# A hybrid encoder layer on one core: the feed-forward stage as a list of steps in a written order

## The chip, the cores and the metric

The kernel runs on one core of one Trainium2 chip. The metric is the device time of one execution in microseconds, as the median of several runs. The engines are named as the profile names them: PE (TensorE; its weight loads are a row of their own, PEld), DVE (VectorE), ACT (ScalarE), POOL (GpSimd) and SP (SyncE, which here only issues transfers). "PEclk" is the share of its full clock that TensorE was granted.

## The reference, cut to what matters

One layer works on a sequence of 256 tokens of width 2048, all in float32. First comes a mixer of two attention groups, whose output is added to x. Then the feed-forward part, which the change is about:

```python
def conv_ffn(h, w_up_l, conv_w_l, conv_b_l, w_down_l):
    u = h @ w_up_l                                   # 2048 -> 2 * 5632
    u = depthwise_causal_conv(u, conv_w_l) + conv_b_l  # width 3, one filter per column
    gate, val = jnp.split(u, 2, axis=-1)
    return (jax.nn.silu(gate) * val) @ w_down_l      # 5632 -> 2048

h = rms_norm(x, ffn_norm)
x = x + conv_ffn(h, w_up, conv_w, conv_b, w_down)
```

The convolution adds, for each column and token, that token's value and the two tokens' before it, each times a weight of the column: three taps and a bias.

## The kernel before, in words

**Two numbers for one.** TensorE multiplies a rounded form of float32 (`float32r`). To keep the precision, every operand is held as a high part (rounded) and a low part (the rest), and a product is made of three: high by high, high by low, low by high. So each weight tile of 1 MB (128 partitions by 2048 values) is loaded into a raw buffer (`load`, L198), cast to its high part on ScalarE (L208), and its low part is the difference of the two, on VectorE (L209). `split` (L204) does the last two. In the feed-forward stage there are four raw buffers and three each for the high and low parts.

**Up pieces and products.** In the up projection two 128-column tiles of `w_up` (a pair) are multiplied by all of h. A pair takes two up pieces, each with one weight tile: eight steps of k, in each two matmuls of 512 columns (L252, high weights by h's high and low part side by side) and two of 256 (L257, low weights by h's high part). The pair's accumulator `pu` comes from a pool of two. When it is complete, `summed` adds its two halves (copy on ScalarE at L268, addition on VectorE at L269), L603 scales the tokens into `up`, and the three taps follow: the last one with the bias on ScalarE (L607), the other two as fused multiply-and-add on VectorE (L612), for each 128-row half alone, so four per pair. When gate and value are both there, SiLU (L783), their product (L784), its high part g (L786) and low part (L787) follow.

**Parts.** The 44 tiles of gate (and of value) are cut into a first part of four tiles and five of eight (`FFN_PARTS`). A part of eight takes 16 up pieces. While one part goes through the up projection, the down projection of the part before runs between its up pieces. For the first part and the last it is done plainly (`down_plain`). For the four parts between, it is done by a scheme of seven products instead of eight (`down_in_seven`, L666): for each of two blocks of 1024 output columns, seven products of 12 matmuls each (L683), so 14 per part. It needs sums and differences of weight tiles (`w_sum`, L715, L722, L728, L739, on VectorE) and of blocks of gate times value (`combinations`, L644: four operations of 256 columns at L652 to L655 on tiles of tag t2, then a high part at L657 and a low part at L658). Each product's result is added to x at once (L692). These four parts' products run during the up projections of the parts after them, which are called loaded parts here. After the last part comes its own down projection, eight pieces of 24 matmuls (L760 to L762), with additions to x (L766) and the stores.

**What sets the order.** Only TensorE's instructions are in the order of the program (L772). On the other queues a scheduler chooses the order from its own cost model and from priorities: `weights` and the down products' loads and splits are moved ahead by 200 instructions (`AHEAD`), the readouts and the work on gate and value by 400. How many products stand between the up pieces is set by a pace, 14 of 16 in the loaded parts but 4 of 16 for the first plain part:

```python
        pace = 4 if n_part == 1 else 14
        for f in range(f_lo, f_hi, 2):
            gate = up_pair(f, "gate", 3, f == f_hi - 2)
            val = up_pair(NFT + f, "val", 1, f == f_hi - 2)
```

What is left of the products at a part's end is emitted before the next part begins.

**The start of the stage.** x is complete when the last output projection has been added (L564). Its last 512 columns are transposed and split into hT (L148, L153, L154, in `next_rows`) by a generator that `step()` advances after each up piece, and h's scale per token (`rstd2`) is applied only later, at L603.

**Projections.** Before the feed-forward stage, `token_major` (L222) makes the products of the attention projections and of the output projection, with three matmuls (L237, L238, L239) per k and token tile in the order high by high, high by low, low by high.

Of the kernel before, what the change touches and what calls it, by code (L numbers as in the profile page):

```python
# [14 lines left out]
P = 128  # L15
D = 2048
# [27 lines left out]
def hybrid_layer(  # L44
# [176 lines left out]

    def token_major(lhs, w, k0, nk, c0, cols, pieces=None, before=None):  # L222

        acc = psa.tile([P, NT, 512], F32, name="acc", tag="acc")
        k = 0
        for n in pieces or [4] * (nk // 4):
            if before:
                before(k, n)
            hi, lo = weights(rows_of(w, k0 + k, n, c0, cols), n, cols)
            for i in range(n):  # L230
                first, last = k + i == 0, k + i == nk - 1
                lh = lhs(k + i)
                for t in range(NT):
                    lhi = lh[:, 0, t * P : (t + 1) * P]
                    llo = lh[:, 1, t * P : (t + 1) * P]
                    o = acc[:, t, :cols]
                    nc.tensor.matmul(o, lhi, hi[:, i, :], start=first, stop=False)  # L237
                    nc.tensor.matmul(o, lhi, lo[:, i, :], start=False, stop=False)  # L238
                    nc.tensor.matmul(o, llo, hi[:, i, :], start=False, stop=last)  # L239
            k += n  # L240
            step()
        return acc
# [330 lines left out]
    R = None  # L573
# [15 lines left out]
    n_up = 0  # L589

    def convolution_parameters():
# [4 lines left out]

    def convolved(ps, f0, tag, bufs):

        nonlocal n_up
        u = up[n_up % 2]  # L600
        n_up += 1
        t2 = summed(ff, ps, "t2")
        dve.tensor_tensor(u[:, :, 2:], t2, R.unsqueeze(1).to_broadcast([P, 2, S]), op=ALU.mult)  # L603
        a = ff.tile([P, 2, S], F32, name=tag, tag=tag, bufs=bufs)
        for j in range(2):
# [5 lines left out]
            for w in range(2):  # L611
                dve.scalar_tensor_tensor(  # L612
                    a[:, j, :], u[:, j, w : w + S], ccol[:, w, f : f + 1], a[:, j, :],
                    op0=ALU.mult, op1=ALU.add,
                )
        return a


    behind = deque()
    n_behind, pace = 0, 0  # L620

    def step():
        nonlocal n_behind
        for g in list(waiting):
            if next(g, g) is g:
                waiting.remove(g)
        n_behind += pace
        while behind and n_behind >= 16:
            if next(behind[0], behind) is behind:
                behind.popleft()  # L630
            else:
                n_behind -= 16

    def up_pair(f0, tag, bufs, soon):

        nonlocal R
        acc = feature_major(wu, f0 * P, psa, "acc")
        if R is None:
            R = in_every_partition(dg2, 2, const)
            convolution_parameters()  # L640
        with tc.high_priority(offset=2 * AHEAD) if soon else nullcontext():
            return convolved(acc, f0, tag, bufs)

    def combinations(g1, g2):  # L644


        a11, a21 = g1[:, :, :P], g1[:, :, P:]
        a12, a22 = g2[:, :, :P], g2[:, :, P:]
        s = ff.tile([P, 2, 4, 2, P], F32R, name="s", tag="s")
        t = [ff.tile([P, 2, 2, P], F32, name="t2", tag="t2") for _ in range(2)]  # L650
        t5, s2, s4, t7 = t[0][:, 0], t[0][:, 1], t[1][:, 0], t[1][:, 1]
        dve.tensor_tensor(t5, a21, a22, op=ALU.subtract)  # L652
        dve.tensor_tensor(s2, t5, a11, op=ALU.subtract)
        dve.tensor_tensor(s4, a12, s2, op=ALU.add)
        dve.tensor_tensor(t7, a11, a21, op=ALU.subtract)  # L655
        for i in range(2):
            act.copy(s[:, 0, 2 * i : 2 * i + 2], t[i])  # L657
            dve.tensor_tensor(  # L658
                s[:, 1, 2 * i : 2 * i + 2], t[i], f32(s[:, 0, 2 * i : 2 * i + 2]), op=ALU.subtract
            )  # L660
        return s

    def store(t, c0):
        nc.sync.dma_start(of[t * P : (t + 1) * P, c0 : c0 + 512], xt[t][:, c0 : c0 + 512])

    def down_in_seven(f0, pairs, sums, c0):  # L666


        w11, w12 = (rows_of(wd, f0, 4, c0 + i * 512, 512) for i in range(2))
        w21, w22 = (rows_of(wd, f0 + 4, 4, c0 + i * 512, 512) for i in range(2))  # L670

        def of_pairs(h, t):
            return lambda a, part, j: pairs[2 * h + a][:, part, j, t * P : (t + 1) * P]

        def of_sums(q):
            return lambda a, part, j: sums[a][:, part, q, j, :]

        def product(bank, first, lhs, parts):
            hi, lo = parts
            for i in range(4):  # L680
                a, j = divmod(i, 2)
                for n, (l, r) in enumerate(((0, hi), (0, lo), (1, hi))):
                    nc.tensor.matmul(  # L683
# [4 lines left out]
        def add(t, half, bank, op=ALU.add):  # L688
            c = c0 + 512 * half
            to = xt[t][:, c : c + 512]  # L690
            with tc.high_priority(offset=2 * AHEAD):
                dve.tensor_tensor(to, to, bank, op=op)  # L692
# [168 lines left out]
```

## Time and profile before

| | us |
|---|---|
| median of 3 runs (1159.28 to 1160.48) | 1160.47 |
| the profiled execution | 1159.43 |
| its span, first to last instruction | 1157.7 |
| TensorE busy | 1123.5 |
| VectorE busy | 888.9 |
| ScalarE busy | 608.2 |
| moved by DMA | 219.77 MB, mean 190 GB/s |

A line of a group or of the timeline names the program's line, the engine, the operation, and out<-in by tile name. In the timeline the first number is the start and the second the length, with the engine's idle time before it in brackets and what ended that. In a table of stretches each row is a stretch of the span, its length, the busy time of PE, PEld, DVE, ACT and POOL with the number of instructions, the granted clock, the share of the DMA engines and their rate. A line of waits is: who <- for whom, total us, how often, the longest. A busy TensorE is not TensorE at its peak, since the end of a matmul is modelled; its rate is read from start to start.

### The profile page before, as it was taken

The numbers are of one execution on the slowest core, as the hardware profiler recorded it, in microseconds if no ns is written. First come the engines' busy times: TensorE is split into PE (matmuls) and PEld (weight loads), VectorE is DVE, ScalarE is ACT, GpSimd is POOL, SyncE is SP. The second block draws the span as 40 slices with busy tenths as digits, with TensorE's granted clock in tenths as the row PEclk, the third lists the DMA queues.
The fourth block names the chain that finished last, engine by engine and source line by source line (L and its number), as shares of the span: only waits on it lengthen the run. The fifth ranks groups of instructions, "written<-read, shape, count | busy, mean of one in ns | idle before, by whom it ended". The sixth has DMA issues, their size and how long they took to land.

```text
span 1157.7 us, 14490 instructions
## 1 busy us (share of the span) xinstructions
PE 1123.5 (97%) x5906; PEld 964.0 (83%) x5906; DVE 888.9 (77%) x972; ACT 608.2 (53%) x664; POOL 0.2 (0%) x4
## 2 busy tenths in 40 slices
PE   7999999999999989999999998999899998999988
PEld 6998888888888878888888887888788887888866
DVE  5646656555465676777899998999999999999983
ACT  5644445345564555554555555465655565565551
POOL 0000000000000000000000000000000000000000
PEclk9999999999999999999999998999999999999999
DMA  7666545555444395555557573665856565576641
GB/s 235 206 217 197 182 147 182 164 164 166 158 150 147 107 309 178 195 197 183 183 182 242 194 242 122 213 224 182 267 168 209 193 218 182 182 255 207 230 163 55
DMA packets 166763, 219.77 MB, mean 190 GB/s; under 512 B 3864, under 2 KB 117674, under 8 KB 166698
## 3 DMA queue, kind: packets, MB, share of 16 engines
q1 hardware_dynamic: 166698, 218.86, 58.1%
q8 instruction: 46, 0.75, 0.3%
q14 instruction: 19, 0.16, 0.0%
HBM read 216.75 MB, written 2.10 MB: 189 GB/s over the span
## 4 chain that ended last, share of the span: by engine, by line
PE 92%; DVE 3%; ACT 2%; DMA 1%; issue 1%; SPq 0%; DVEq 0%; ACTq 0%
PE pu L252 33%; PE pu L257 16%; PE acc L238 7%; PE acc L237 7%; PE acc L239 7%; PE bank_a L683 7%; PE bank_b L683 4%; PE bank_c L683 2%; ACT w_hi L208 2%; DVE w_lo L209 2%; PE acc L760 1%; PE acc L761 1%; PE acc L762 1%; PE bank_a L760 1%; PE bank_a L761 1%
## 5 line engine op out<-in xcount | busy, mean ns | idle before, releaser
L209 DVE TENSOR_TENSOR w_lo<-w_raw,w_hi 128x2048 fp32r<-128x2048 f32 (+2 forms) x204 | 449.6, 2207 | 193.4 <-ACT w_hi L208 192.6
L208 ACT CAST w_hi<-w_raw 128x2048 fp32r<-128x2048 f32 (+2 forms) x204 | 375.8, 1842 | 326.3 <-PE pu L252 103.4
L252 PE MATMUL pu<-hT,w_hi 128*128 128x512 f32 x1664 | 528.5, 399 | 14.4 <-DVE t L269 13.4
L257 PEld LDWEIGHTS pu<-hT,w_lo 128*128 128x128 f32 x1664 | 315.4, 190 | 76.3 <-DVE w_lo L209 2.0
L257 PE MATMUL pu<-hT,w_lo 128*128 128x256 f32 x1664 | 329.3, 279 | 1.5 <-DVE w_lo L209 1.5
L252 PEld LDWEIGHTS pu<-hT,w_hi 128*128 128x128 f32 x1664 | 260.3, 191 | 20.5 <-issue 14.6
L237 PE MATMUL acc<-w_hi,hT 128*128 128x512 f32 (+1 forms) x320 | 119.9, 375 | 0.0
L238 PE MATMUL acc<-w_lo,hT 128*128 128x512 f32 (+1 forms) x320 | 119.0, 372 | 0.8 <-DVE w_lo L209 0.8
L239 PE MATMUL acc<-w_hi,hT 128*128 128x512 f32 (+1 forms) x320 | 118.6, 371 | 0.0
L208 ACT CAST w_hi<-w_sum 128x2048 fp32r<-128x2048 f32 x24 | 45.9, 1914 | 79.9 <-DVE w_sum L715 43.4
L238 PEld LDWEIGHTS acc<-w_lo,hT 128*128 128x128 f32 x320 | 60.4, 189 | 9.9 <-DVE w_lo L209 1.7
L239 PEld LDWEIGHTS acc<-w_hi,hT 128*128 128x128 f32 x320 | 60.4, 189 | 8.7
L237 PEld LDWEIGHTS acc<-w_hi,hT 128*128 128x128 f32 x320 | 60.5, 189 | 8.2
L209 DVE TENSOR_TENSOR w_lo<-w_sum,w_hi 128x2048 fp32r<-128x2048 f32 x24 | 54.9, 2290 | 3.2 <-ACT w_hi L208 2.8
L683 PE MATMUL bank_a<-w_hi,g 128*128 128x512 f32 x128 | 42.1, 390 | 0.0
L683 PE MATMUL bank_b<-w_hi,s 128*128 128x512 f32 x128 | 42.1, 390 | 0.0
L683 PE MATMUL bank_a<-w_hi,s 128*128 128x512 f32 x128 | 42.1, 390 | 0.0
L612 DVE SCALAR_TENSOR_TENSOR val<-up,ccol,val 128x256 f32<-128x256 f32 x88 | 38.1, 480 | 0.2
L268 ACT COPY t<-pu 128x512 f32<-128x512 f32 x52 | 30.2, 580 | 15.1 <-PE pu L257 14.2
L612 DVE SCALAR_TENSOR_TENSOR gate<-up,ccol,gate 128x256 f32<-128x256 f32 x88 | 37.5, 479 | 0.7 <-ACT gate L607 0.7
L237 PE MATMUL acc<-w_hi,oT 128*128 128x512 f32 x96 | 38.0, 396 | 0.0
L239 PE MATMUL acc<-w_hi,oT 128*128 128x512 f32 x96 | 37.5, 390 | 0.0
(186 smaller groups left out, 1172.9 us busy)
## 6 DMA issues: line engine op xcount, KB each, us to landing
w_raw<-in_w_up_dram SPq DMA_DIRECT2D x88, 1024.0 KB, 5.5
w_raw<-in_w_down_dram SPq DMA_DIRECT2D x52, 1024.0 KB, 5.2
w_raw<-in_w_in_dram SPq DMA_DIRECT2D x36, 1024.0 KB, 5.3
w_raw<-in_w_out_dram SPq DMA_DIRECT2D x16, 1024.0 KB, 5.3
w_raw<-in_w_in_dram SPq DMA_DIRECT2D x12, 688.0 KB, 4.2
w_raw<-in_w_in_dram SPq DMA_DIRECT2D x8, 512.0 KB, 4.2
out_dram<-x SPq DMA_DIRECT2D x8, 256.0 KB, 2.4
x<-in_x_dram SPq DMA_DIRECT2D x3, 512.0 KB, 6.2
```

What stands on the lines that cost most here:

```text
L208: act.copy(hi[:, :n], raw[:, :n])
L209: dve.tensor_tensor(lo[:, :n], raw[:, :n], f32(hi[:, :n]), op=ALU.subtract)
L237: nc.tensor.matmul(o, lhi, hi[:, i, :], start=first, stop=False)
L238: nc.tensor.matmul(o, lhi, lo[:, i, :], start=False, stop=False)
L239: nc.tensor.matmul(o, llo, hi[:, i, :], start=False, stop=last)
L252: nc.tensor.matmul(acc[:, j, :], hi[:, i, j * P : (j + 1) * P], hT[:, k].rearrange("p a b -> p (a b)"), start=k == 0, stop=False,)
L257: nc.tensor.matmul(acc[:, j, S:], lo[:, i, j * P : (j + 1) * P], hT[:, k, 0, :], start=False, stop=k == KT - 1,)
L268: act.copy(t2, acc[:, :, S:])
L612: dve.scalar_tensor_tensor(a[:, j, :], u[:, j, w : w + S], ccol[:, w, f : f + 1], a[:, j, :], op0=ALU.mult, op1=ALU.add,)
L683: nc.tensor.matmul(bank, lhs(a, l, j), r[:, i, :], start=first and i + n == 0, stop=i == 3 and n == 2, skip_group_check=not first,)
L760: nc.tensor.matmul(acc[t], g[:, 0, ts], hi[:, i, :], start=first, stop=False)
L761: nc.tensor.matmul(acc[t], g[:, 0, ts], lo[:, i, :], start=False, stop=False)
```

## The change

It does four things.

1. `token_major` and the down projections no longer take high by high, high by low and low by high one after the other for each k. A new helper `in_three` first goes through all k with the high weights, and then through all k with the low weights. The number of matmuls is the same.
2. The convolution's first two taps become scaled copies on ScalarE (four per pair, 256 columns each) into two tiles of tag t2, which VectorE adds with two operations of 512 columns.
3. The sums and differences of blocks are made in place in the four gate tiles of a part, all of them after its last value, instead of into t2 tiles after its third and fourth pair. There are four gate buffers instead of three, and seven of g2 instead of eight.
4. The stage becomes a list of steps (one for an up piece or a product), each with a load, perhaps a weight sum, a split, its matmuls and what follows on them. One loop emits them: at step n the load of step n+6, the split of step n+2, the weight sum of step n+4, the matmuls of n. What follows on a finished pair is a generator which is advanced twice in each step, so that its work is spread over some five steps. PE, DVE, ACT and SP are all held to this order. The steps before the first matmuls (n < 0) have a raised priority against the work before the stage. In a loaded part the first product stands after the third up piece, and then one after each up piece. `step()`, with the last transposes of x, is called ahead of the matmuls of the first up piece; the transposes of the convolution's parameters stand before the third.

The diff, cut (the generators of `up_pieces` and `down_plain` make steps in the same way as those shown; `product` and the list of seven keep the sums, banks and signs they had):

```diff
+    def in_three(accs, parts, n, lhs, starts, stops):
+        hi, lo = parts
+        order = [(i, l, hi) for i in range(n) for l in range(2)] + [(i, 0, lo) for i in range(n)]
+        for j, (i, l, r) in enumerate(order):
+            for t, o in enumerate(accs):
+                nc.tensor.matmul(
+                    o, lhs(i, l, t), r[:, i, :], start=starts and j == 0,
+                    stop=stops and j == 3 * n - 1, skip_group_check=len(accs) == 1 and not starts,
+                )
...
     def convolved(ps, f0, tag, bufs):
-        t2 = summed(ff, ps, "t2")
-        dve.tensor_tensor(u[:, :, 2:], t2, R.unsqueeze(1).to_broadcast([P, 2, S]), op=ALU.mult)
+        u = up[f0 // 2 % 2 ^ (f0 >= NFT)]
+        yield
+        t2 = ff.tile([P, 2, S], F32, name="t2", tag="t2")
+        act.copy(t2, ps[:, :, S:])
+        dve.tensor_tensor(t2, ps[:, :, :S], t2, op=ALU.add)
+        R = tokens[0].unsqueeze(1).to_broadcast([P, 2, S])
+        dve.tensor_tensor(u[:, :, 2:], t2, R, op=ALU.mult)
+        yield
+        yield
         a = ff.tile([P, 2, S], F32, name=tag, tag=tag, bufs=bufs)
+        taps = [ff.tile([P, 2, S], F32, name="tap", tag="t2") for _ in range(2)]
...
-            for w in range(2):
-                dve.scalar_tensor_tensor(
-                    a[:, j, :], u[:, j, w : w + S], ccol[:, w, f : f + 1], a[:, j, :],
-                    op0=ALU.mult, op1=ALU.add,
+        for w in range(2):
+            for j in range(2):
+                f = f0 + j
+                act.activation(
+                    taps[w][:, j, :], u[:, j, w : w + S], AF.Copy, scale=ccol[:, w, f : f + 1]
                 )
+        yield
+        for tap in taps:
+            dve.tensor_tensor(a, a, tap, op=ALU.add)
         return a
...
+    def val_follows(part, ps, f0):
+        a = yield from convolved(ps, NFT + f0, "val", 1)
+        gate = part.gates[(f0 - part.f_lo) // 2]
+        dve.tensor_tensor(gate, gate, a, op=ALU.mult)
+        yield
+        g2 = ff.tile([P, 2, 2, S], F32R, name="g2", tag="g2", bufs=7)
+        act.copy(g2[:, 0], gate)
+        yield
+        dve.tensor_tensor(g2[:, 1], gate, f32(g2[:, 0]), op=ALU.subtract)
+        part.pairs.append(g2)
+        if f0 == part.f_hi - 2 and len(part.pairs) == 4:
+            both = [(part.gates[n], part.gates[n + 2]) for n in range(2)]
+            for g1, g2 in both:
+                a11, a21 = g1[:, :, :P], g1[:, :, P:]
+                a12, a22 = g2[:, :, :P], g2[:, :, P:]
+                dve.tensor_tensor(a11, a11, a21, op=ALU.subtract)
+                dve.tensor_tensor(a21, a21, a22, op=ALU.subtract)
+                dve.scalar_tensor_tensor(a22, a11, -1.0, a22, op0=ALU.mult, op1=ALU.subtract)
+                dve.tensor_tensor(a12, a12, a22, op=ALU.add)
+            yield
+            for gs in both:
+                s = ff.tile([P, 2, 2, 2, S], F32R, name="s", tag="s")
+                for i, g in enumerate(gs):
+                    act.copy(s[:, 0, i], g)
+                part.sums.append(s)
+            yield
+            for s, gs in zip(part.sums, both):
+                for i, g in enumerate(gs):
+                    dve.tensor_tensor(s[:, 1, i], g, f32(s[:, 0, i]), op=ALU.subtract)
...
+        elif last.f_hi - last.f_lo < 8:
+            behind = [down_plain(last, c) for c in range(0, D, 512)]
+            at_piece = range(3, 16, 4)
+        else:
+            behind = [g for c in (0, 1024) for g in [down_in_seven(last, c)] * 7]
+            at_piece = range(16 - len(behind), 16)
+        behind = deque(behind)
+        for i, piece in enumerate(pieces):
+            next(piece)
+            if i in at_piece:
+                next(behind.popleft())
...
-    ctx.enter_context(tc.manual_schedule(engines={mybir.EngineType.PE}))
+    ctx.enter_context(
+        tc.manual_schedule(
+            engines={mybir.EngineType.PE, mybir.EngineType.DVE, mybir.EngineType.Activation, mybir.EngineType.SP}
+        )
+    )
+    LOAD, SUM, SPLIT = 6, 4, 2
+    following = []
+
+    def follow():
+        following[:] = [g for g in following if next(g, g) is not g]
+
+    for n in range(-LOAD, len(steps) + 8):
+        def at(ahead, what):
+            if 0 <= n + ahead < len(steps) and steps[n + ahead][what]:
+                return steps[n + ahead][what]()
+
+        with tc.high_priority(offset=2 * AHEAD) if n < 0 else nullcontext():
+            if n >= 0:
+                step()
+                if n == 2:
+                    parameters()
+            at(LOAD, 0)
+            follow()
+            at(SPLIT, 2)
+            follow()
+            at(SUM, 1)
+            at(0, 3)
+            follows = at(0, 4)
+            if follows:
+                following.append(follows)
```

More of the change, by code (lines that the diff above doesn't have):

```diff
@@ L634, in up_pair @@
[L634 to L659, printed above, removed]
-            )
-        return s
```

280 lines of the change are left out of this document (135 added, 145 removed).

## The prediction

> **What bounds the kernel now.** I read the page's busy shares first, then the waits, then stretches of the feed-forward stage (411.67 us to the end).
>
> ```profile
> span 1157.7 us, 14490 instructions
> PE 1123.5 (97%) x5906; PEld 964.0 (83%) x5906; DVE 888.9 (77%) x972; ACT 608.2 (53%) x664; POOL 0.2 (0%) x4
> ```
> ```profile
> 697.87:832.59 134.72, 130.25 (x682) 111.55 (x681) 126.30 (x121) 75.21 (x66) 0.00 (x0) 0.97 0.62 203
> 832.59:966.57 133.98, 129.51 (x682) 110.91 (x681) 126.29 (x121) 75.20 (x67) 0.00 (x0) 0.97 0.62 204
> 966.57:1100.09 133.52, 129.05 (x682) 110.51 (x681) 126.31 (x121) 75.20 (x66) 0.00 (x0) 0.99 0.61 205
> ```
> ```profile
> PE pu L252 <- DVE t L269: 13.4, 3, 4.5
> PE acc L760 <- DVE t L269: 4.5, 1, 4.5
> PE acc L238 <- DVE w_lo L209: 0.8, 2, 0.4
> ```
>
> TensorE is the bound at 97%. A loaded part of the feed-forward stage (16 up pieces and 14 products of the part before) takes 134.1 us, the mean of the three stretches (columns: stretch and its length, then PE, PEld, DVE, ACT). VectorE is busy for 126.3 of it, ScalarE for 75.2. TensorE loses four waits of 4.5 us, one at each loaded part's end. What one such wait is made of, on VectorE's queue and then TensorE's:
>
> ```profile
> 697.97 0.42 DVE L652 TENSOR_TENSOR t<-gate 128x256 f32<-128x256 f32 x1
> ...
> 699.10 0.42 DVE L654 TENSOR_TENSOR t<-gate,t 128x256 f32<-128x256 f32 x1
> 699.82 2.29 DVE L209 TENSOR_TENSOR w_lo<-w_raw,w_hi 128x2048 fp32r<-128x2048 f32 x1 [0.30 <-ACT w_hi L208]
> 702.03 0.69 DVE L787 TENSOR_TENSOR g<-gate,g 128x512 fp32r<-128x512 f32 x1
> 702.63 1.29 DVE L658 TENSOR_TENSOR s<-t,s 128x512 fp32r<-128x512 f32 x2
> 703.84 0.68 DVE L692 TENSOR_TENSOR x<-x,bank_a 128x512 f32<-128x512 f32 x1
> 704.43 1.28 DVE L269 TENSOR_TENSOR t<-pu,t 128x512 f32<-128x512 f32 x2
> ```
> ```profile
> 705.27 0.77 PE L252 MATMUL pu<-hT,w_hi 128*128 128x512 f32 x1 [4.47 <-DVE t L269]
> ```
> ```profile
> 703.00:708.00 5.00, 2.73 (x9) 2.39 (x10) 5.00 (x8) 2.96 (x7) 0.00 (x0) 0.64 0.65 210
> 708.00:712.00 4.00, 4.00 (x15) 3.42 (x15) 4.00 (x9) 1.06 (x2) 0.00 (x0) 0.59 0.00 0
> 712.00:716.00 4.00, 4.00 (x25) 3.48 (x24) 2.51 (x6) 2.37 (x3) 0.00 (x0) 1.00 0.00 0
> ```
>
> The next up pair's accumulator is free only after the readout L269, which stands behind block sums, a weight split and g. After the wait the granted clock is 0.64 and 0.59 for some microseconds, and only then 1.00.
>
> TensorE's own need per part:
>
> ```profile
> 727.69 2.73 PE bank_c L683 x12
> 735.98 2.73 PE bank_b L683 x12
> ```
>
> A product takes 2.73 us and the next starts 8.29 later, so an up piece takes 8.29 - 2.73 = 5.56. A part needs 16 x 5.56 + 14 x 2.73 = 127.2. The loss is 134.1 - 127.2 = 6.9 per part: 4.5 waiting, 2.4 at the low clock. With four waits, about 27.5 us are to be had.
>
> **The change part by part.** VectorE's costs are taken from start to start, since its instructions overlap by some 0.1 us:
>
> ```profile
> 642.40 1.67 DVE L612 SCALAR_TENSOR_TENSOR gate<-up,ccol,gate 128x256 f32<-128x256 f32 x4
> 643.99 0.69 DVE L603 TENSOR_TENSOR up<-t,R 128x512 f32<-128x512 f32 x1
> ...
> 653.51 0.69 DVE L269 TENSOR_TENSOR t<-pu,t 128x512 f32<-128x512 f32 x1
> 654.11 2.28 DVE L209 TENSOR_TENSOR w_lo<-w_raw,w_hi 128x2048 fp32r<-128x2048 f32 x1
> 656.31 2.29 DVE L715 TENSOR_TENSOR w_sum<-w_raw 128x2048 f32<-128x2048 f32 x1
> ```
>
> A low split or a weight sum costs 2.20, a 512-wide operation 0.60, a tap 0.40, a 256-wide block sum (697.97 to 699.10, three) about 0.38.
>
> *Taps.* Four fused taps (1.6 us) leave VectorE for each of the eight up pairs of a part, two 512-wide additions (1.2) come: -3.2 per part, so 126.3 becomes 123.1, still under TensorE's 127.2. ScalarE gets 32 scaled copies per part. Their nearest row:
>
> ```profile
> 660.52 1.91 ACT L208 CAST w_hi<-w_raw 128x2048 fp32r<-128x2048 f32 x1
> 662.32 1.09 ACT L607 ACTIVATE gate<-up,ccol 128x256 f32<-128x256 f32 x2
> ```
>
> At 0.545 that is +17.4: ScalarE goes from 75.2 to 92.6 of 127, not a bound by its sum. [...]
>
> *Block sums in place.* Same count and widths, one of four in the fused form; the two t2 buffers they held go to the taps. Nothing on VectorE within 0.1 us per pair. The last part's sums, which nobody reads, stay; its own products come with 11 us to spare, so they hide.
>
> *Low weights last.* No matmul added or removed. A product can start with its low split up to 8 matmuls (1.8 us) late. In the projections the row above shows only 0.8 us of such waits: 0 taken, bounds -1 and +1.
>
> *The fixed order.* For each step, loads go out six steps ahead, weight sums four, splits two; a finished up pair is read out, convolved, gated and split piecewise over the next four to five steps. The products start after a part's third up piece, so its predecessor's tail has two bare up pieces (11.1 us) as cover: the 4.5 us wait and its clock loss go, -27.5.
>
> What is late next: VectorE in the bunch behind the tail. Its queue, step by step:
> - third up piece: split 2.2, last g 0.6, eight block sums 3.0, readout and scaling of a pair 1.2 = 7.0
> - product 1: split 2.2, four splits of block sums 2.4, weight sum 2.2 = 6.8
> - up piece: split 2.2, tap additions 1.2, addition to x 0.6 = 4.0
> - product 2: split 2.2, readout and scaling 1.2, weight sum 2.2 = 5.6
> - up piece: split 2.2, addition to x 0.6 = 2.8
> - product 3: split 2.2, taps 1.2, gate times value 0.6, weight sum 2.2 = 6.2
>
> That is 32.4 us against 3 x 8.29 = 24.9 of matmuls: VectorE starts the next step 7.5 behind. There g and x (1.2) stand before the split (2.2) of the up piece two steps on, due after 8.29: 7.5 + 3.4 - 8.29 = 2.6 us late. Elsewhere in the part, laid out the same way, no backlog passes 5 us, and with one addition to x before the split 8.29 - 2.2 - 0.6 = 5.5 would do. For handovers I add 0.4: TensorE waits 3.0 us per part, in pieces short enough to keep the clock (below, 1.54 did). Bounds: 0 if the backlog is covered, 6.9 if the clock loss comes with it. Four parts: +12.0.
>
> *Loads.* As many loads, in fixed order on SP's queue over four raw buffers. The stores at the end stand behind the last load, with nothing behind them.
>
> ```profile
> w_raw<-in_w_up_dram SPq DMA_DIRECT2D x88, 1024.0 KB, 5.5
> w_raw<-in_w_down_dram SPq DMA_DIRECT2D x52, 1024.0 KB, 5.2
> ```
>
> The second operand of the first weight sum gets a buffer after the split in the third up piece (1 + 3.6 + 2.2 = 6.8 after that piece starts, allowing 1 for its cast), lands at 12.0, and VectorE wants it at 7.0 + 2.4 + 2.2 = 11.6 or a little later: just in time. 0 taken, bounds 0 and the rival below.
>
> *The start.* The last transposes move ahead of the first up piece; in the trace that piece covers them:
>
> ```profile
> 411.67 0.63 PE L252 MATMUL pu<-hT,w_hi 128*128 128x512 f32 x2
> 413.84 0.51 PE L257 MATMUL pu<-hT,w_lo 128*128 128x256 f32 x2 [1.54 <-DVE w_lo L209]
> ...
> 419.06 0.38 PE L148 MATMUL ps_x<-cs,x 128*128 128x128 f32 x2
> ```
> ```profile
> 413.70 1.41 DVE L564 SCALAR_TENSOR_TENSOR x<-acc,rg,x 128x512 f32<-128x512 f32 x2
> ```
>
> The transposes for the convolution's parameters stay between the second and the third up piece, at no change. The last ones of x now wait for L564 until 415.1, which is 3.4 us of idle TensorE where 1.5 and a few fractions stood: +0.5, bounds -0.5 and +2.9, the upper if the clock falls as after 4.47. [...]
>
> **The sum.** The profiled execution took 1159.43 us (1.7 beside its span; 1.0 under the median of 1160.47). 1159.4 - 27.5 + 12.0 + 0.5 = 1144.4; with half the distance to the median, 1145.
>
> **The rivals.**
> 1. *The tail is fully covered.* VectorE hides its bunch and TensorE runs at 127.2 per part: 1159.4 - 27.5 + 0.5 = 1132. For it: 123.1 is under 127.2. Against: the 32.4 in 24.9.
> 2. *Loads late.* Two loads in flight share the queue: 2.1 MB at the page's highest slice (309 GB/s, below) take 6.8 us instead of 5.5, 1.3 more. Four weight sums of a part wait for a load made just before (the first two of each column block): 5.2 us on VectorE, 1145 + 4 x 5.2 = 1166 at worst, 1155 if only the first block's two count.
>
> ```profile
> GB/s 235 206 217 197 182 147 182 164 164 166 158 150 147 107 309 178 195 197 183 183 182 242 194 242 122 213 224 182 267 168 209 193 218 182 182 255 207 230 163 55
> ```
>
> 3. *ScalarE's round trip, slower.* The tap additions stand at the head of VectorE's step and wait for six activations (6 x 0.545 = 3.3) behind a cast (1.9) and VectorE's own scaling; splits and sums queue behind them. VectorE has 127.2 - 123.1 = 4.1 us per part free. If each of eight pairs makes it wait w, a part lasts 123.1 + 8w: as now at w = 1.4. At 2 us: 139.1, so 4 x 5.0 slower: 1180. For it: an in-order queue at 97% fill. Against: the casts and activations (5.2) fit an up piece (5.56), and with a backlog VectorE comes late anyway. [...]
> 4. *It does not do what it says:* the order leaves some wait at each part's end, 1159 to 1161.
>
> **How the numbers follow.** Forecast 0.58, first rival 0.08, loads 0.10 (a fifth of it no change or slower), round trip 0.19, nothing 0.05. About 0.2% (2.3 us) is what a measurement of this kernel can tell from no change. Faster 0.74, same 0.06, slower 0.20. The forecast's own range is 1134 to 1155 (wait per part 0.5 to 5.5, start up to +2.9). For 8 in 10 it reaches from 1132 to 1164, into the loads case and the mildest round trip.
>
> **What would show it.** Right: no 4.5 us wait of pu on t, granted clock near 1.00 at the part ends; one wait of 2 to 3 us per part on w_lo at the up piece after the third product; fused taps gone, VectorE's busy time down by 44 x 0.4 = 18 us, ScalarE's up by 176 x 0.545 = 96. Wrong: VectorE waiting long for tap (round trip) or w_sum for raw (loads), TensorE waits spread over a whole part, or over 4 us idle at the start.

## The result, and the profile after

| | before | after |
|---|---|---|
| median, us | 1159.88 (1159.10 to 1160.48, 4 runs) | 1143.10 (1142.68 to 1143.22, 4 runs) |
| the profiled execution | 1159.43 | 1142.68 |
| its span | 1157.7 | 1140.9 |

The ratio is 0.9855, with a 95% interval of 0.9838 to 0.9872: about 1.5% faster, 1.9 us from the predicted 1145.

The page of the kernel after gives the busy times, the granted clock in 40 slices, and the scaled copies on ScalarE:

```profile
span 1140.9 us, 14688 instructions
PE 1119.5 (98%) x5906; PEld 958.5 (84%) x5906; DVE 874.2 (77%) x884; ACT 681.1 (60%) x840; POOL 0.2 (0%) x4
PEclk9999999999999999999999999999999999999999
...
L642 ACT ACTIVATE tap<-up,ccol 128x256 f32<-128x256 f32 x176 | 74.6, 496 | 0.0
```

TensorE is busy 4.0 us less than before although its matmuls are as many: the low clock at the part ends is gone. VectorE loses 14.7 us and ScalarE gains 72.9; the 176 taps are busy for 74.6, that is 0.42 us each (one alone lasts 496 ns, but neighbours overlap).

The stretches of the loaded parts, cut close to each part's first product (stretch and length, then PE, PEld, DVE, ACT, POOL, granted clock, DMA):

```profile
588.80:718.67 129.87, 128.30 (x681) 109.19 (x681) 123.83 (x105) 87.92 (x99) 0.00 (x0) 1.00 0.63 211
718.67:848.72 130.05, 128.30 (x681) 109.18 (x681) 124.00 (x105) 87.90 (x99) 0.00 (x0) 1.00 0.64 210
848.72:978.78 130.06, 128.33 (x682) 109.20 (x681) 124.01 (x105) 87.91 (x99) 0.00 (x0) 1.00 0.63 210
```

A part now takes 130.05 us instead of 134.1. If the fourth loaded part, which has no row here, gains as much as these three, that is 16.2, nearly all of the 16.75 between the two profiled executions; about 1 of the 1.5 us that the start gains (below) is lost again in small pieces elsewhere. The clock is 1.00 throughout.

TensorE's waits in the feed-forward stage of the kernel after, then where its weight loads wait in the part that begins at 718.67, then all of VectorE's waits in the loaded parts:

```profile
PE pu L717 <- DVE w_lo L209: 6.1, 7, 1.4
PE ps_x L148 <- DVE x L573: 1.6, 2, 1.3
```
```profile
730.36 0.30 PEld L717 LDWEIGHTS pu<-hT,w_lo 128*128 128x128 f32 x2 [0.63 <-DVE w_lo L209]
738.89 0.30 PEld L717 LDWEIGHTS pu<-hT,w_lo 128*128 128x128 f32 x2 [0.39 <-DVE w_lo L209]
748.82 0.30 PEld L717 LDWEIGHTS pu<-hT,w_lo 128*128 128x128 f32 x2 [1.79 <-DVE w_lo L209]
```
```profile
DVE w_lo L209 <- ACT w_hi L208: 17.8, 12, 2.5
```

The 4.5 us waits of `pu` on `t` are gone. In their place stand three short ones on a low split, after the second, the third and the fourth product: 0.63 + 0.39 + 1.79 = 2.8 us per part, which is also what lies between 130.05 and the 127.2 of need. (TensorE's own row, 6.1 us in the stage, shows less, since the ends of its matmuls are modelled.) VectorE waits neither for a tap nor for a load, so the rivals of the round trip and of late loads did not come about. Its one wait is for the high cast ahead of a split, 4.4 us per part and never in the bunch of work around the first products: over a whole part VectorE has some time left, in the bunch it has none.

The start of the stage, before and after:

```profile
428.90 0.70 PE L252 MATMUL pu<-hT,w_hi 128*128 128x512 f32 x2
```
```profile
412.95 0.33 PE L148 MATMUL ps_x<-cs,x 128*128 128x128 f32 x1 [1.28 <-DVE x L573]
413.61 0.98 PE L148 MATMUL ps_x<-cs,x 128*128 128x128 f32 x7 [0.33 <-DVE x L573]
```
```profile
427.44 0.71 PE L712 MATMUL pu<-hT,w_hi 128*128 128x512 f32 x2
```

The third up piece starts at 428.90 before and at 427.44 after: the start gained 1.5 us.

### The profile page after: what moved, and what is told of

Its sections match the earlier page's. It is cut to its first block, busy times and chain, and to the rows that moved or that the text cites. A ratio compares the mean times of both kernels' runs of the same rounds, so it can differ in the third digit from the quotient of the medians.

```text
span 1140.9 us, 14688 instructions
## 1 busy us (share of the span) xinstructions
PE 1119.5 (98%) x5906; PEld 958.5 (84%) x5906; DVE 874.2 (77%) x884; ACT 681.1 (60%) x840; POOL 0.2 (0%) x4
## 4 chain that ended last, share of the span: by engine, by line
PE 77%; DVE 16%; issue 5%; ACT 1%; DMA 1%; SPq 0%; DVEq 0%; ACTq 0%
PE acc L229 26%; PE pu L712 20%; PE pu L717 10%; DVE w_lo L209 9%; PE bank_a L229 7%; PE pu L261 5%; PE pu L266 3%; PE bank_b L229 2%; DVE w_sum L775 2%; DVE x L731 1%; DVE w_raw L775 1%; ACT w_hi L208 1%; DVE val L647 1%; DVE t L626 1%; PE ps_x L148 1%
## 5 line engine op out<-in xcount | busy, mean ns | idle before, releaser
L712 PE MATMUL pu<-hT,w_hi 128*128 128x512 f32 x1408 | 441.8, 395 | 0.0
L229 PE MATMUL acc<-w_hi,hT 128*128 128x512 f32 (+1 forms) x640 | 143.3, 374 | 0.0
L229 PEld LDWEIGHTS acc<-w_hi,hT 128*128 128x128 f32 x640 | 114.2, 190 | 16.9
L261 PE MATMUL pu<-hT,w_hi 128*128 128x512 f32 x256 | 81.4, 399 | 0.0
L642 ACT ACTIVATE tap<-up,ccol 128x256 f32<-128x256 f32 x176 | 74.6, 496 | 0.0
L229 PE MATMUL acc<-w_lo,hT 128*128 128x512 f32 (+1 forms) x320 | 74.5, 371 | 0.0
L229 PE MATMUL bank_a<-w_hi,g 128*128 128x512 f32 x192 | 47.0, 390 | 0.0
L229 PE MATMUL acc<-w_hi,oT 128*128 128x512 f32 x192 | 46.3, 393 | 0.0
L229 PEld LDWEIGHTS acc<-w_hi,oT 128*128 128x128 f32 x192 | 35.4, 188 | 7.0
L229 PEld LDWEIGHTS bank_a<-w_hi,g 128*128 128x128 f32 x192 | 34.5, 188 | 6.1
L635 ACT ACTIVATE val<-up,ccol 128x256 f32<-128x256 f32 x44 | 24.0, 594 | 25.8 <-DVE up L628 25.8
```

Of the source, the lines that this page charges most:

```text
L229: nc.tensor.matmul(o, lhs(i, l, t), r[:, i, :], start=starts and j == 0, stop=stops and j == 3 * n - 1, skip_group_check=len(accs) == 1 an ...
L261: nc.tensor.matmul(acc[:, j, :], hi[:, i, j * P : (j + 1) * P], hT[:, k].rearrange("p a b -> p (a b)"), start=k == 0, stop=False,)
L635: act.activation(a[:, j, :], u[:, j, 2:], AF.Identity, scale=ccol[:, 2, f : f + 1], bias=ccol[:, 3, f : f + 1],)
L642: act.activation(taps[w][:, j, :], u[:, j, w : w + S], AF.Copy, scale=ccol[:, w, f : f + 1])
L712: nc.tensor.matmul(acc[:, j, :], hi[:, i, j * P : (j + 1) * P], hT[:, k].rearrange("p a b -> p (a b)"), start=k == 0, stop=False,)
```

## The experiments

My theory was the prediction's: the written order covers the tail (most of the gain), VectorE's freed time is worth the rest, and the order of the matmuls in a product is worth nothing. The rivals are in the expectations. A run's ratio is to executions of the kernel before that were timed together with it.

**1. The change with the taps back on VectorE.**

```diff
-        taps = [ff.tile([P, 2, S], F32, name="tap", tag="t2") for _ in range(2)]
-        (four act.activation into taps, two dve.tensor_tensor adding them)
+        for j in range(2):
+            f = f0 + j
+            for w in range(2):
+                dve.scalar_tensor_tensor(a[:, j, :], u[:, j, w : w + S], ccol[:, w, f : f + 1], a[:, j, :], ...)
```

> The changed kernel with the two taps back on VectorE as fused operations (four of 0.40 us per pair instead of two additions of 0.60). Main theory (the written order removes the wait at the part ends, and the moved taps leave VectorE the room to keep that order): VectorE gets 8 x 0.4 = 3.2 us more per loaded part, 0.8 of it inside the bunch, and the rest of the part has no slack left; a part of 130.05 becomes about 132.5, so 1143.1 + 4 x 2.5 = 1153 us (1149 to 1156). Rival 'the order alone does it, the taps are beside the point': 1143 to 1145. Rival 'the taps carry the gain': back to about 1160.

1153.11 us (1152.92 to 1155.68), ratio 0.9938 (0.9919 to 0.9958). TensorE's waits on the low splits nearly double:

```profile
PE pu L715 <- DVE w_lo L209: 11.1, 8, 1.8
```

In the written order the taps on ScalarE are worth 1153.1 - 1143.1 = 10 us, as the main theory had it. VectorE has 3.2 us more work per part and is later by about as much. Part of the loss is the clock: after three of its four longest waits, 1.80 us each, the granted clock falls to 0.50 (after the first from 621 to 623).

**2. The kernel before with the taps alone.** The same edit the other way round, in the scheduler's order.

> The kernel before with only the taps moved: four scaled copies on ScalarE and two additions on VectorE per pair, in the scheduler's order. Main theory: the 4.5 us wait at the part end stays, because the block sums, a weight split and g still stand ahead of the readout; at most 0.8 us of taps leaves that queue: 1157 us, 1153 to 1162, with the clock still falling to about 0.6 after each wait. Rival 'the taps carry the gain' (VectorE 3.2 us per part lighter, all of it on the path): 1159.9 - 4 x 3.2 = 1147 us or less.

1157.37 us (1152.37 to 1159.13), ratio 0.9967 (0.9951 to 0.9983). As expected, there is a small gain: the waits at the part ends shrink but stay. (The rows are of an execution of 1159.13 us; three of the ten took 1152.4 to 1153.2.)

```profile
PE pu L252 <- DVE t L269: 8.3, 3, 3.1
PE acc L764 <- DVE t L269: 2.6, 1, 2.6
```

The tap tiles stand in tag t2 here, which the readouts use too. Run 11 shows what that can cost; the taps alone with buffers of their own were not run, so this is not the price of the taps by themselves.

**3. The kernel before with the low weights last alone.** `in_three` for the three nests of matmuls, and nothing else.

> The kernel before with only the order of the matmuls in products and projections changed, low weights last. Main theory: the wait at the part end is a wait for an accumulator, not for a low split, and the projections waited 0.8 us for low splits in all: 1159 to 1160 us. Rival 'the earlier release of the high weights lets the casts start earlier and shortens the part': 1155 or less.

1144.41 us (1143.89 to 1146.27), ratio 0.9861 (0.9843 to 0.9879). My theory fell: the part that I had put at nothing gives, alone, almost the whole gain. The waits at the part ends:

```profile
PE pu L259 <- DVE t L276: 2.8, 3, 0.9
```

Two things change with this order, and runs 5 to 7 tell them apart: a product can start before its low split is there (tolerance), and its last matmul with the high weights comes four matmuls earlier, so that ScalarE may overwrite that buffer with the next cast (release).

**4. The change with the interleaved order back.**

```diff
-        order = [(i, l, hi) for i in range(n) for l in range(2)] + [(i, 0, lo) for i in range(n)]
+        for i in range(n):
+                for m, (l, r) in enumerate(((0, hi), (0, lo), (1, hi))):
```

> The changed kernel with the old order inside each product (high by high, high by low, low by high for each k). Main theory: all waits for low splits that the changed kernel still has are of up pieces (pu), none of a product, so the tolerance of 1.8 us is not drawn on: 1143 to 1145 us. Rival 'the tolerance is what lets products start in time': a product in the bunch waits up to 1.8 us, 4 x 1.8 = 7, 1150 us.

1146.22 us (1145.61 to 1146.55), ratio 0.9875 (0.9856 to 0.9894), 3.1 above the change and just above the main theory's range. The waits of the up pieces are as after (6.0 in seven), and the loaded parts are as long as after, 129.99 against 130.05:

```profile
PE pu L717 <- DVE w_lo L209: 6.0, 7, 1.4
PE ps_x L148 <- DVE x L573: 3.1, 2, 2.7
```
```profile
721.52:851.51 129.99, 128.28 (x682) 109.19 (x681) 123.96 (x105) 88.43 (x99) 0.00 (x0) 1.00 0.63 211
```

All of the 3.1 stands at the start of the stage. The transposes of x wait 1.5 us longer there, the granted clock then falls to 0.50 (stretch 416 to 418), and the third up piece starts at 430.48 instead of 427.44. VectorE's addition to x, in the change and in this run:

```profile
412.15 1.40 DVE L573 SCALAR_TENSOR_TENSOR x<-acc,rg,x 128x512 f32<-128x512 f32 x2
```
```profile
413.65 1.40 DVE L573 SCALAR_TENSOR_TENSOR x<-acc,rg,x 128x512 f32<-128x512 f32 x2
```

In the written order the low weights last are worth about 3 us, at the start, and nothing in the loaded parts. In the scheduler's order they are worth 15, in the loaded parts (130.20 us each in run 3, against 134.1). There both remedies remove the same waits, so their gains do not add.

**5, 6, 7. Tolerance and release apart.** Three orders of the twelve matmuls in the kernel before; each is run 3 with one line changed.

```diff
 # 5: low weights in the middle: some tolerance, high buffer released at the end
+        order = [(i, 0, r) for r in (hi, lo) for i in range(n)] + [(i, 1, hi) for i in range(n)]
 # 6: one high matmul moved to the very end: more tolerance, released at the end
+        order = order[: 2 * n - 1] + order[2 * n :] + order[2 * n - 1 : 2 * n]
 # 7: one low matmul moved to the very front: no tolerance, released early
+        order = order[2 * n : 2 * n + 1] + order[: 2 * n] + order[2 * n + 1 :]
```

> The kernel before with the low weights in the middle third of each product: high by high, then high by low, then low by high. A product may start with its low split 4 matmuls (0.9 us) late instead of 8 (1.8), and the high weights are released at the product's end again, as in the kernel before. New theory N (low weights last lets VectorE's queue put low splits later and the readout of the accumulator sooner; what counts is the lateness a product bears): most of the gain of 15.4 us stays, 1144 to 1152 us. Rival R (what counts is that the high buffers come free a third of a product sooner, so the casts start sooner): the gain goes, 1157 to 1161 us.

> The kernel before with seven high-weight matmuls, then the four low ones, then the last high one in each product: it bears a low split 1.6 us late, but its high weights are released only at its end, as in the kernel before. Theory R (the gain of low weights last in the scheduler's order comes from the earlier release of the high buffers): 1157 to 1161 us, with the 4.5 us waits of pu on t. Theory N (it comes from the lateness that a product bears; 0.9 us was too little): 1144 to 1150 us.

> The kernel before with one low matmul first, then all eight high ones, then the other three low ones in each product: it bears no lateness of the low split, but its high weights are released three matmuls (0.7 us) before its end. Theory R (earlier release of the high buffers): 1144 to 1152 us. Theory N (lateness borne): 1157 to 1161 us, with the 4.5 us waits of pu on t.

Low in the middle: 1158.88 us (1158.60 to 1161.93), ratio 0.9991 (0.9981 to 1.0001). One high matmul last: 1159.95 (1157.23 to 1161.27), 1.0001 (0.9991 to 1.0011). One low matmul first: 1152.41 (1151.00 to 1155.23), 0.9945 (0.9927 to 0.9962), 0.4 above the range that the release theory had given. ScalarE's waits show why. Its casts that wait for a product to leave their buffer, in the loaded parts of the kernel before, and of the run with one high matmul last:

```profile
ACT w_hi L208 <- PE bank_a L683: 9.7, 12, 1.0
...
ACT w_hi L208 <- PE bank_b L683: 8.3, 8, 1.0
```
```profile
ACT w_hi L208 <- PE bank_a L228: 9.8, 12, 1.0
...
ACT w_hi L208 <- PE bank_b L228: 8.4, 8, 1.0
```

Both sum to 18 us. In the run with the low weights last (run 3) the same list has no wait of a cast for `bank_a` or `bank_b` at all. Whichever order keeps a high matmul at the end keeps these waits and the 4.5 us wait at each part's end, whatever its tolerance. What an earlier release does to the chain at the part's end, ScalarE's queue in the kernel before and in run 3:

```profile
692.58 1.91 ACT L208 CAST w_hi<-w_raw 128x2048 fp32r<-128x2048 f32 x1 [1.04 <-PE bank_b L683]
697.87 1.92 ACT L208 CAST w_hi<-w_raw 128x2048 fp32r<-128x2048 f32 x1 [3.38 <-PE pu L252]
699.69 0.61 ACT L786 CAST g<-gate 128x512 fp32r<-128x512 f32 x1
...
703.35 1.19 ACT L268 COPY t<-pu 128x512 f32<-128x512 f32 x2 [0.21 <-DVE s L658]
```
```profile
693.28 1.91 ACT L208 CAST w_hi<-w_raw 128x2048 fp32r<-128x2048 f32 x1
695.09 0.62 ACT L782 CAST g<-gate 128x512 fp32r<-128x512 f32 x1
...
700.79 0.57 ACT L275 COPY t<-pu 128x512 f32<-128x512 f32 x1
```

The cast of g comes 4.6 us earlier and the readout's copy 2.6, though an up piece's cast starts at 692.58 and at 693.28, nearly the same moment. In the kernel before, one more cast, which waits 3.38 us for an up piece, stands ahead of the cast of g; in run 3 that cast stands behind it. So the queues are not the old ones shifted: with nothing edited but the matmuls' order, the scheduler chose another one. That it did so because its model saw the buffers freed earlier is likely, not shown. That release is needed in the scheduler's order is shown. How much of it acts on the chip, and how much through the order that the scheduler then chooses, these runs do not separate.

Release alone does not give all. In run 7 the part-end waits are as small as in run 3, but a new wait stands in the products. In run 3 the same product of the first of these parts starts at 730.40 while its low split runs to 731.16, so there the tolerance is drawn on. VectorE's order differs in run 7 too (a weight sum stands ahead of that split), so the 2.8 us are not the price of the tolerance alone:

```profile
PE bank_b L228 <- DVE w_lo L209: 8.0, 3, 2.8
PE pu L260 <- DVE t L277: 2.8, 3, 0.9
```

**8. Filler in the wait.** The kernel before, with 18 matmuls whose results nobody reads at the end of the last four parts (4.24 us), to keep TensorE busy and price the low clock.

```diff
+        if n_part >= 2:
+            filler = psf.tile([P, 512], F32, name="filler", tag="a")
+            for _ in range(18):
+                nc.tensor.matmul(filler, hT[:, 0, 0, :P], hT[:, 0].rearrange("p a b -> p (a b)"), start=True, stop=True)
```

> The kernel before with 18 matmuls of 512 columns that nobody reads (18 x 0.2275 = 4.1 us) on TensorE's queue at the end of each of the last four parts, where it waits 4.5 us. Theory: the wait itself stays, filled, but the clock no longer falls after it: 4 x 2.4 = 9.6 us less, 1150 us (1148 to 1153). Rival 'the low clock is not set off by the idle time' or 'the filler delays the next up piece': 1159 or more.

1154.11 us (1152.98 to 1157.29), ratio 0.9953 (0.9941 to 0.9966). That is a little above the theory's range. One part, with the clock at 1.00:

```profile
784.59:916.99 132.40, 131.89 (x700) 112.64 (x699) 125.90 (x121) 75.17 (x67) 0.00 (x0) 1.00 0.63 207
```

That is 1.7 us less than 134.1, and not 2.4. The clock after 4.5 us of waiting is lower for a while (0.64 and then 0.59 from 703 to 712 in the kernel before) and costs about 1.7 us: useless matmuls shortened the kernel.

**9. The change with the products one up piece later.** The first product comes after the fourth up piece, the last two follow each other.

```diff
-            at_piece = range(16 - len(behind), 16)
+            at_piece = [*range(3, 16), 15]
```

> The changed kernel with the products of a part starting after its fourth up piece instead of the third, and the last two in a row. Theory (the waits of 2.85 us per part that are left come from the bunch on VectorE at the start of a part): one more bare up piece of 5.56 us stands against it, the largest backlog falls from 7.5 to about 6 us, of the four times 2.85 us about 0.7 each are left: 1143.1 - 4 x 2.1 = 1134.5 us (1133 to 1139). Rival 'VectorE is simply full, 124.0 of 130.05, and the waits go where the work goes': 1142 to 1145.

1142.41 us (1141.69 to 1142.65), ratio 0.9848 (0.9830 to 0.9865). The gain that I expected did not come, and the rival's time did. The waits stay, in one more place:

```profile
PE pu L717 <- DVE w_lo L209: 7.4, 8, 1.3
```

Moving the work by a piece moves the backlog. In the change VectorE is busy for 124.0 us of 130.05 and waits 4.4 for casts, in a queue in strict order, and the 0.7 us by which this run is under the change is less than a measurement can tell.

**10. The change with the weight sums on GpSimd.**

```diff
-                dve.tensor_tensor(mem[into], mem[a], mem[b], op=ALU.add)
+                nc.gpsimd.tensor_tensor(mem[into], mem[a], mem[b], op=ALU.add)
```

> The changed kernel with the eight weight sums of a part on GpSimd, which is idle, instead of VectorE. Theory (VectorE's load is what is left to win): VectorE has 17.6 us less per part, no wait for a low split stays: 1143.1 - 11.4 = 1132 us, if one sum takes GpSimd under 8.3 us and leaves VectorE's speed alone. Rival 'the two engines get in each other's way at the buffers, or the sum on GpSimd is too slow': low splits longer than 2.2 us, or casts waiting for w_sum, 1145 us or more.

1211.70 us (1210.49 to 1211.85), ratio 1.0444 (1.0425 to 1.0463): slower than before. One sum on GpSimd's timeline, then VectorE's beside it, then TensorE's waits:

```profile
741.37 4.96 POOL L775 TENSOR_TENSOR w_sum<-w_raw 128x2048 f32<-128x2048 f32 x1 [32.98 <-DMA w_raw<-in_w_down_dram]
```
```profile
739.57 2.28 DVE L209 TENSOR_TENSOR w_lo<-w_raw,w_hi 128x2048 fp32r<-128x2048 f32 x1
741.77 5.90 DVE L647 TENSOR_TENSOR gate<-gate,tap 128x512 f32<-128x512 f32 x2
```
```profile
PE pu L717 <- DVE w_lo L209: 47.8, 24, 5.4
```

Two additions that take 1.48 us together elsewhere in this run took 5.90 while GpSimd worked until 746.33. VectorE gave away 2.2 us of work per sum and lost more than that waiting beside it: in a part (717.02 to 864.06) it is busy for 134.05 us instead of 124.0, although eight sums (17.6) have left it.

**11, 12. Low weights last and taps on ScalarE, in the scheduler's order.** The first puts the two tap tiles in tag t2, as the change does. The second gives them two buffers of their own, and takes the room from g2.

```diff
 # both: the kernel before with in_three, and the taps as in the change
+        taps = [ff.tile([P, 2, S], F32, name="tap", tag="t2") for _ in range(2)]
 # the second, against the first
-        taps = [ff.tile([P, 2, S], F32, name="tap", tag="t2") for _ in range(2)]
+        taps = [ff.tile([P, 2, S], F32, name="tap", tag="tap") for _ in range(2)]
-                g2 = ff.tile([P, 2, 2, S], F32R, name="g2", tag="g2", bufs=8)
+                g2 = ff.tile([P, 2, 2, S], F32R, name="g2", tag="g2", bufs=7)
```

> The kernel before with low weights last and the taps on ScalarE, that is the change without its written order, its steps and its block sums in place. If the written order adds nothing over a scheduler that has the other two: 1136 to 1143 us (VectorE 3.2 us per part lighter than in the kernel with low weights last alone, 1144.4, which had 2.9 us of waits per part left). If the order is what makes use of the moved taps: 1143 to 1148, waits on t or g staying at the part ends.

> The kernel before with the low weights last and the taps on ScalarE, as in the run of 1181.6 us, but the two tap tiles have a pair of buffers of their own instead of the tag t2 that the readouts and the block sums use; the room comes from g2, seven buffers instead of eight, as many as the changed kernel has. Theory S (in that run the readout of an accumulator had to wait until both taps of the pair before it had left t2, so the shared buffers made the loss): the long waits of pu on the readout go and the time falls to that of the low weights last alone or below, 1136 to 1148. Rival (the scheduler's order is the loss: it puts the tap additions where VectorE has to wait for ScalarE, whatever buffer they are in): 1165 to 1182, VectorE's waits on tap stay at about 10 us, TensorE's waits of pu on t stay above 15. Between 1148 and 1165 both have a share.

With t2 shared: 1181.59 us (1180.71 to 1184.11), ratio 1.0197 (1.0181 to 1.0213), slower than before, which neither side had expected. With buffers of their own: 1141.07 us (1140.18 to 1142.20), ratio 0.9835 (0.9819 to 0.9852), the lowest median of all, without the written order. Waits of the first (TensorE's, then ScalarE's copy of a readout, then VectorE's):

```profile
PE pu L259 <- DVE t L276: 26.4, 9, 4.8
```
```profile
ACT t L275 <- DVE val L626: 5.3, 3, 1.8
```
```profile
DVE gate L626 <- ACT tap L622: 9.8, 5, 2.0
```

The readout of an accumulator is copied into a t2 tile, and there were two of them for the readouts, the taps and the block sums. The copy waits for the tap additions before it, and TensorE waits for the readout. With own buffers the copy's wait for an addition is gone. TensorE's waits of the second, and one of its stretches from part to part, cut at the first up matmul behind the wait:

```profile
PE pu L259 <- DVE t L276: 2.3, 3, 0.8
```
```profile
702.57:831.43 128.86, 127.79 (x681) 109.19 (x681) 122.65 (x105) 87.48 (x99) 0.00 (x0) 1.00 0.64 212
```

That is 128.9 per part against 130.05 in the written order, and 127.2 of need. It gives some of that back where the written order is better, at the start of the stage, where it waits 2.0 us for hT, and 2.0 us for g in the last part's down projection. So the loss of the eleventh run came from the shared buffers, and a written order is not needed to avoid it. In the change the taps share t2 with the readouts too, but the block sums, made in place, no longer do; what that is worth by itself no run shows.

## Why the prediction was right, and where it was not

*What bounds the kernel.* Right. The loss sat in the waits at the part ends and the low clock behind them. After, the part ends are covered, the clock is 1.00, and a part is 4.05 us shorter; predicted was 6.9 - 3.0 = 3.9. Run 4 shows that the written order with the moved taps does this in the loaded parts without the low weights last.

*The low clock* was 2.4 of the 6.9 in the working. Filler prices it at 1.7, seen alone, so some 0.7 of the 2.4 was something else, which no run isolates.

*The bunch on VectorE* was put at 3.0 us per part at one place and measured at 2.8 at three. The working has the delay at the up piece two steps beyond the step behind the third product, and there stands the largest, 1.79; the last part of the prediction named the up piece after the third product, which waits only 0.39. The mechanism was right. A sum of work against time over three products does not say where the first pieces of it come late. That the sizes agree to 0.2 us owes something to luck: the eight block sums take 3.4 us instead of 3.0 (712.25 to 715.68), a readout and its scaling 1.3 instead of 1.2, and the 0.4 for handovers was set by hand.

*Taps.* The additions came as predicted. VectorE's busy time fell by 14.7 instead of 18, in a part from 126.3 to 124.0, 2.3 instead of 3.2. Run 1, which differs from the change in the taps alone, is busy for 127.2 and 127.7 in two of its parts, so the taps themselves are worth 3.2 to 3.7; some 1.3 come back with the written order and the sums in place. (Run 12, with the same taps in the scheduler's order, is busy for 122.65.) The timelines show where: in the change each of a part's eight readouts has its scaling, which needs it, right behind it, 0.72 us from start to start (717.88, 718.60), where neighbours that do not need each other stand 0.60 apart. That is about 1.0, an estimate. The block sums in place, 0.45 apart (712.25, 712.70) where most stood 0.35 apart, can be the rest. ScalarE rose by 73 instead of 96: the nearest row in the trace (0.545 us) was an activation that takes a scale and a bias from ccol, the taps take a scale alone and took 0.42; whether that makes the difference no run shows. Some of it was in the reading: from start to start two of that row take 0.98 us (683.63 to 684.61 before), 0.49 each, and four taps 1.60 (721.28 to 722.88 after), 0.40 each. Run 1 puts the moved taps at 10 us, because VectorE's queue is the one that is late: without the move TensorE's waits for low splits are 11.1 us instead of 6.1.

*Loads.* Right at 0: VectorE has no wait for a load in the loaded parts.

*The start.* Put at +0.5, measured at -1.5, and the 2 us do not come from the written order. I had left the addition to x at the time that it has before, 413.70. With the written order and the old order of matmuls (run 4) it does stay there, at 413.65; the transposes wait 2.72 + 0.33 us, against 3.4 forecast, the clock falls to 0.50, and the third up piece starts 1.6 us later than before, within my bounds. With the low weights last the addition comes at 412.15, the transposes wait 1.28 + 0.33 us, and the clock stays at 1.00. In the chain ahead of it the cast that waits for the output projection's matmuls starts at 398.13 instead of 400.01, and the split, the load and the cast behind it are earlier too; VectorE's order differs there as well, and no run tells the two apart.

*Low weights last, 0 with bounds of -1 and +1.* This step failed, through what it left out. I looked only at what a late low split would cost (tolerance), and not at what the order frees. In the change it is worth 3.1 us (run 4), outside my bounds, all of them at the start; in the loaded parts 0 was right. Alone, in the scheduler's order, it is worth 15 (run 3). The total held because in the loaded parts the written order and the low weights last remove the same waits: whichever is there first takes the gain. Without them the change would have come to 1146.2, 1.2 above the forecast instead of 1.9 below it.

*The written order, -27.5 less 12.* Right as a difference between these two kernels, but not as a cause that only an order by hand can supply. Low weights last, taps on ScalarE and two buffers for them get 1141.07 in the scheduler's order, where the change gets 1143.10. Their ratios' intervals overlap, so I do not call one faster. Nor does the order carry the gain without the moved taps: run 1 has the written order, the sums in place and the low weights last, and takes 1153.1, while run 3, which has only the low weights last, takes 1144.4. Beside the low weights last, the written order and the sums in place together cost 8.7 us there. The written order with neither the taps nor the low weights last was not run.

The forecast was the likeliest case, the range held, and the size of the whole was right to 1.9 us. The mechanism of the loaded parts was right too, within 0.2 us per part. The attribution among the four parts was not.

## What to carry to other kernels

Ask of every order of matmuls not only what it waits for but which buffer it frees, and when: the same twelve matmuls with the high weights first gave 15 us in the scheduler's order, and an order that bears nearly as late a low split but keeps one high matmul for the end gave nothing. And a remedy is worth what the others leave: with the queues in a written order the same edit gave 3. When a step moves to another engine, count the buffers that it takes; two taps in a tag that the readouts use turned a gain of 18 us into a loss of 22 in the scheduler's order. And price a change's parts alone and undone: two remedies for one wait look like a sum and are not.

## What the runs showed of the hardware

*GpSimd's sums and VectorE's operations.* In run 10 two VectorE additions took 5.90 us instead of 1.48 beside a GpSimd sum of 4.96. From 588 to 1160 us of that run a low split of a loaded tile lasts 2.94 us in the mean, where the change has 2.29, the scaling of a readout 1.67 instead of 0.69, and gate's addition of a tap 1.23 instead of 0.69. The 86 additions with one operand in an accumulator kept their 0.68 us. So did some others (the low part of g 0.68, val's addition of a tap 0.69). What sets the longer ones apart no run shows.

*How long a pause the clock bears.* In the feed-forward stage the trace of before has no pause between 1.54 and 4.47 us, and 1.54 leaves the clock at 1.00. (It has one of 2.79 us, for a load, 5.5 us after the kernel's start; the clock in its rows is 1.00, but the first matmuls there start 0.4 to 0.7 us apart, where later ones start 0.23 apart, so it settles nothing.) The experiments fill the gap. Run 12, stretches of TensorE around a pause of 1.96 us at the start of the stage and around one of 1.97 us in the last down projection (stretch, length, PE busy, granted clock, DMA):

```profile
422.00:424.00 2.00, 0.47 (x2) 1.00 1.09 336
424.00:426.00 2.00, 2.00 (x8) 0.50 1.10 350
...
1102.00:1104.00 2.00, 0.18 (x1) 1.00 1.03 399
1104.00:1106.00 2.00, 1.84 (x7) 1.00 0.13 47
```

One halves the clock (0.50) and the other leaves it (1.00). After pauses of 2.06 and 3.04 us in run 11 it was 0.50 too, after the 1.28 us of the kernel after it stayed 1.00. In run 1 three pauses of 1.80 us halved it and a fourth of 1.80 did not. So between 1.80 and 2 us it went either way in these runs, and what decides it none of them shows.
